# Second feed-forward block of a decoder layer: other chunk orders, six more mixed chunks, dense activations, another order of the last banks

## The chip, the cores and the metric

The kernel runs on one core of one Trainium2 chip. The metric is the device time of one execution in microseconds (us). It was run three times before the change: 2109.17, 2108.28 and 2108.98 us, a median of 2108.98 us.

## The reference

One layer of a decoder, for 256 tokens behind 16 learned meta tokens, in float32, with a width of 2048 and a hidden width of 5632:

```python
u = rms_norm(h, ffn1_norm_g[l])
h = h + 0.5 * swiglu(u, ffn1_w_gate[l], ffn1_w_up[l], ffn1_w_down[l])
u = rms_norm(h, mix_norm_g[l])
z = u @ w_in[l]
...                       # sparse attention, gated short convolution, merge
h = h + merged @ w_out[l]
u = rms_norm(h, ffn2_norm_g[l])
h = h + 0.5 * swiglu(u, ffn2_w_gate[l], ffn2_w_up[l], ffn2_w_down[l])
return h[:, N_META:]
```

with `swiglu(x, g, u, d) = (silu(x @ g) * (x @ u)) @ d`. The change lies almost wholly in the second `swiglu`, of which only the 256 tokens are computed.

## The kernel before, in words

Three stages follow each other: the first feed-forward block (`ffn_features`), the mixer (attention, convolution, merge, output projection), and the second feed-forward block (`ffn_tokens`). TensorE computes float32 products out of two rounded halves: each operand is split into a high part (`hi`, ScalarE, L175) and a rest (`lo`, VectorE, L176), and one product is three matmuls, hi by hi, hi by lo, lo by hi. In `ffn_tokens` this is `trio` (L408, L409, L410): the activations are the stationary operand of 128x128, the weights stream past in 512 columns. L409 is the matmul that reads the `lo` weights.

**Stream.** All weights pass through one `Stream`. It loads chunks of 128x2048 words from HBM on the SP queue into raw buffers (three, and a fourth, `raws`, in the second block), splits them piece by piece into `whi` and `wlo` (four buffers of 1024 columns each), and hands the pieces to TensorE in order. When TensorE's program comes to piece number `at`, `Stream.next` writes, in this order, the work put for the start of that piece (`first`), the split of the piece three further on, and the work put for its end (`waiting`):

```python
self.run(self.first, self.at)
if self.steps:
    self.steps.pop(0)()
self.split(self.at + 1 + self.ahead)
self.run(self.waiting, self.at)
```

So the order of each engine's list is fixed by piece numbers. `put(fns, slots)` counts in half pieces from now: slot 15 is the end of piece 7. A tuple of such slots for each kind of work stands in `LAG`. The split of a piece needs the buffer of the piece four before, which TensorE must have finished; this bounds how far VectorE and ScalarE can be ahead.

**The second block.** The 5632 hidden features are cut into eleven tiles of 512, in two groups of six and five. A tile multiplies the 256 tokens with 512 gate and 512 up columns, over 2048 rows: eight chunks of 256 rows (`quads`, with `gu` counting chunks). Behind the tiles of a group come two down passes (`d` = 0 and 2), each into 1024 output columns; their chunks are 256 hidden features each: twelve in the first group, ten in the second. I name the tiles of the first group tile 1 to 6, and the passes down 1 and down 2 (first group) and down 3 and down 4 (second group).

**Plain and mixed chunks.** A plain chunk is eight block products (two token halves, two row halves, two column halves), so 24 matmuls, in two pieces `0` and `1` of 12 matmuls each. A mixed chunk uses seven block products instead (Strassen's scheme in Winograd's form): 21 matmuls in four pieces, `A` (6), `B` (3, half a piece wide), `C` (6) and `D` (6). For it the stream loads 128x1536 words of the chunk and 128x2048 words of sums of its blocks. Those weight sums are made earlier, in `job`: load the chunk on the POOL queue, four VectorE additions (L568), store to a scratch tensor in HBM on the POOL queue. 57 such jobs run: 46 in the first block (`JOBS`), eleven in the merge part of the mixer. The sums of activations are made in `combos`: five additions (L702 to L706), then a split on ScalarE (L688) and VectorE (L689). Where these sums are kept, for the down passes, is in `homes`.

`MIXED` names the mixed chunks of a tile (1, 3, 5, 6; tile 1 has only 5, in `FIRST_MIXED`), `DOWN_MIXED` and `LAST_MORE` those of the down passes (6, 8, 9, 10 in both passes of the first group; 5, 6, 7 in down 3 and 3, 4, 5, 6, 7 in down 4). Within a tile or a pass the chunks run in rising order.

**Ends of tiles and passes.** Behind the last mixed chunk `spread` combines the banks of the extra products (L767 on ScalarE, L768 to L770 on VectorE). A down pass then adds into the residual: four operations of `halves_to` from the combined banks, and four of `gather_down` from the plain ones (all L840, one each of 128x512). In the second group `gather_down` also stores the output columns. `quads` with `tail` set runs the last chunk bank by bank, six matmuls each, in the order (first half of tokens, columns 0), (first, 1), (second, 0), (second, 1); the two banks of columns 0 lie in one tile, `three`.

The activations `act` of the second block lie in rows of 320 words (`PITCH`) of which 256 are used.

## Time and profile before

| | |
|---|---|
| runs, us | 2108.28, 2108.98, 2109.17 |
| span of the profiled execution | 2106.9 us, 2.1 us below the median of the runs |
| instructions | 31863, of which 12731 matmuls |
| DMA | 575.64 MB, mean 273 GB/s |
| first matmul of the second block | at 1418.94 us of the span |

The profile is one execution on the chip: a page with the busy time of each engine, forty equal slices, the DMA queues and the chain of work that ended last, and a trace that can be asked for single rows. PE is TensorE's matmuls, PEld its loads of the stationary operand, DVE is VectorE, ACT ScalarE, SP and POOL issue DMAs. A row of the timeline is: start, duration, engine, line, operation, out<-in with shapes, count, and in brackets the idle time before it with what ended it. Matmuls overlap: each is shown with 0.39 us though the next starts sooner, so PE is read by the starts of its rows and not by its busy time.

### The profile page before, as it was taken

The page shows a single profiled execution, that of the slowest core. Times are in us where ns is not written, and L with a number is a line of the kernel's source. Part 1 is how long each engine was busy: PE and PEld are TensorE (multiplying, and loading weights), DVE is VectorE, ACT ScalarE, POOL GpSimd, SP SyncE. Part 2 cuts the span into 40 slices and gives each one's busy share as a digit, 9 for nine tenths or more (in the row PEclk, how much of TensorE's full clock was granted, in tenths as well). Part 3 has the DMA queues.
Part 4 walks back from the last instruction along what each step waited for, and adds up shares of the span by engine and source line. Part 5 has one row for each costly group of instructions (what it writes and reads, how often), then busy time and mean ns, then how long its engine had stood idle before and what let it go on. Part 6 is the DMA issues. An engine that isn't in the chain of part 4 may idle for free.

```text
span 2106.9 us, 31863 instructions
## 1 busy us (share of the span) xinstructions
PE 2098.8 (100%) x12731; PEld 1889.9 (90%) x12731; DVE 1582.4 (75%) x2144; ACT 1058.9 (50%) x1342; POOL 106.0 (5%) x207
## 2 busy tenths in 40 slices
PE   9999999999999999999999999999999999999998
PEld 9999999999999999889988888888888888888887
DVE  7676766676776766578679678769788896878897
ACT  6444433344444445565444444456575565566654
POOL 0000000000000000000000000011000000000000
PEclk9999999999999999999999999999999999999999
DMA  7788888888888865445468886667988777799865
GB/s 265 260 320 327 324 315 322 311 337 310 322 313 325 328 224 177 164 159 181 152 216 329 323 301 223 219 233 255 314 314 300 281 268 247 282 306 319 306 250 207
DMA packets 85908, 575.64 MB, mean 273 GB/s; under 512 B 10112, under 2 KB 10880, under 8 KB 23808
## 3 DMA queue, kind: packets, MB, share of 16 engines
q1 hardware_dynamic: 64080, 438.34, 58.4%
q0 software_dynamic: 21104, 134.23, 17.1%
q8 instruction: 99, 1.62, 0.3%
q10 hardware_dynamic: 576, 1.05, 0.1%
q14 instruction: 49, 0.40, 0.1%
HBM read 504.90 MB, written 68.68 MB: 272 GB/s over the span
## 4 chain that ended last, share of the span: by engine, by line
PE 98%; DVE 1%; DMA 1%; issue 0%; ACT 0%; DVEq 0%; ACTq 0%
PE three L409 5%; PE three L408 5%; PE three L410 5%; PE pd L375 4%; PE pd L376 4%; PE pd L374 4%; PE pu L374 4%; PE pg L375 4%; PE pg L374 4%; PE pu L375 4%; PE pg L376 4%; PE pu L376 4%; PE pgt L402 3%; PE pgt L404 3%; PE pgt L403 3%; PE one L408 3%
## 5 line engine op out<-in xcount | busy, mean ns | idle before, releaser
L176 DVE TENSOR_TENSOR wlo<-raw,whi 128x1024 fp32r<-128x1024 f32 (+1 forms) x771 | 906.2, 1188 | 464.5 <-ACT whi L175 457.7
L175 ACT ACTIVATE whi<-raw 128x1024 fp32r<-128x1024 f32 (+1 forms) x771 | 786.4, 1030 | 883.4 <-PE pd L375 146.2
L375 PE MATMUL pd<-mid,whi 128*128 128x272 f32 x704 | 201.9, 287 | 0.0
L376 PE MATMUL pd<-mid,wlo 128*128 128x272 f32 x704 | 201.9, 287 | 0.0
L374 PE MATMUL pd<-mid,whi 128*128 128x272 f32 x704 | 201.9, 287 | 0.0
L374 PE MATMUL pu<-act,whi 128*128 128x272 f32 x672 | 192.8, 287 | 0.0
L376 PE MATMUL pu<-act,wlo 128*128 128x272 f32 x672 | 192.7, 287 | 0.0
L376 PE MATMUL pg<-act,wlo 128*128 128x272 f32 x672 | 192.7, 287 | 0.0
L375 PE MATMUL pg<-act,whi 128*128 128x272 f32 x672 | 192.7, 287 | 0.0
L375 PE MATMUL pu<-act,whi 128*128 128x272 f32 x672 | 192.7, 287 | 0.0
L374 PE MATMUL pg<-act,whi 128*128 128x272 f32 x672 | 192.7, 287 | 0.0
L568 DVE TENSOR_TENSOR made<-made 128x512 f32<-128x512 f32 x228 | 156.3, 685 | 0.0
L408 PE MATMUL three<-whi,act 128*128 128x512 f32 x352 | 137.2, 390 | 0.1
L409 PE MATMUL three<-wlo,act 128*128 128x512 f32 x352 | 137.0, 389 | 0.0
L410 PE MATMUL three<-whi,act 128*128 128x512 f32 x352 | 137.0, 389 | 0.0
L376 PEld LDWEIGHTS pd<-mid,wlo 128*128 128x128 f32 x704 | 132.7, 188 | 0.0
L374 PEld LDWEIGHTS pd<-mid,whi 128*128 128x128 f32 x704 | 132.7, 188 | 0.0
L375 PEld LDWEIGHTS pd<-mid,whi 128*128 128x128 f32 x704 | 132.7, 188 | 0.0
L176 DVE TENSOR_TENSOR wlo<-raws,whi 128x1024 fp32r<-128x1024 f32 x92 | 103.5, 1140 | 31.7 <-ACT whi L175 31.0
L374 PEld LDWEIGHTS pu<-act,whi 128*128 128x128 f32 x672 | 126.7, 188 | 0.0
L374 PEld LDWEIGHTS pg<-act,whi 128*128 128x128 f32 x672 | 126.7, 188 | 0.0
L376 PEld LDWEIGHTS pg<-act,wlo 128*128 128x128 f32 x672 | 126.6, 188 | 0.0
(381 smaller groups left out, 4482.7 us busy)
## 6 DMA issues: line engine op xcount, KB each, us to landing
raw<-in_wgu_dram SPq DMA_DIRECT2D x123, 1024.0 KB, 6.4
raw<-in_wd_dram SPq DMA_DIRECT2D x63, 1024.0 KB, 6.7
made<-in_wgu_dram POOLq DMA_DIRECT2D x41, 1024.0 KB, 10.6
made<-made POOLq DMA_DIRECT2D x41, 1024.0 KB, 6.5
raw<-made SPq DMA_DIRECT2D x31, 1024.0 KB, 6.1
raw<-in_wcv_dram SPq DMA_DIRECT2D x24, 1024.0 KB, 4.9
raw<-in_wgc_dram SPq DMA_DIRECT2D x24, 1024.0 KB, 5.1
raw<-in_wga_dram SPq DMA_DIRECT2D x24, 1024.0 KB, 5.4
```

What stands on the lines that cost most here:

```text
L175: nc.scalar.activation(hi[:, :n], raw, AF.Copy)
L176: nc.vector.tensor_sub(lo[:, :n], raw, hi[:, :n].bitcast(F32))
L374: nc.tensor.matmul(ps, whi, xhi, start=first, stop=False)
L375: nc.tensor.matmul(ps, whi, xlo, start=False, stop=False)
L376: nc.tensor.matmul(ps, wlo, xhi, start=False, stop=last)
L402: nc.tensor.matmul(ps, xhi, whi, start=k + i == 0, stop=False)
L403: nc.tensor.matmul(ps, xhi, wlo, start=False, stop=False)
L404: nc.tensor.matmul(ps, xlo, whi, start=False, stop=k + i == n - 1)
L408: nc.tensor.matmul(ps, x(0), w[0], start=first, stop=False)
L409: nc.tensor.matmul(ps, x(0), w[1], start=False, stop=False)
L410: nc.tensor.matmul(ps, x(1), w[0], start=False, stop=last)
L568: getattr(nc.vector, f"tensor_{op}")(to, a, b)
```

## The change

The chunks of tile 1 and of each down pass get an order of their own (`FIRST`, `DOWN`), and `order` takes that list. Two more chunks are mixed in tile 1 (1 and 3), one more in down 1 (4), two more in down 2 (4 and 2), one more in down 4 (2). Their activation sums are all put in the first pass of a group, by longer slot lists; `start` puts the additions and the splits when its time comes. To have room for them, `act` is packed densely (256 words a row) at the front of its tile, and the rest of the tile holds two more sets of sums (`beyond`). 63 weight sums are made in place of 57: 46 in the first block as before, six at the start of the mixer (`MID_JOBS`, in the places where `qT` and half of `cs` lie later, which are therefore allocated later), eleven in the merge part as before. The last chunk's banks run in the order (first, 0), (second, 0), (first, 1), (second, 1), and the output follows them.

```diff
-FIRST_MIXED = 5,
+FIRST_MIXED = 5, 1, 3
+FIRST = 0, 2, 4, 5, 1, 6, 3, 7
-LAST_MORE = 3, 4
-DOWN_MIXED = {6: (6, 8, 9, 10), 5: (5, 6, 7)}
+MID_JOBS = 6
+MID_FROM = 3
+MID_EVERY = 5
+DOWN = {
+    (0, 0): (0, 1, 2, 3, 5, 6, 8, 7, 9, 10, 4, 11),
+    (0, 2): (0, 6, 8, 1, 9, 10, 3, 4, 2, 5, 7, 11),
+    (1, 0): (0, 1, 2, 3, 4, 5, 6, 8, 7, 9),
+    (1, 2): (0, 5, 6, 1, 7, 4, 8, 3, 2, 9),
+}
+DOWN_MIXED = {(0, 0): (6, 8, 9, 10, 4), (0, 2): (6, 8, 9, 10, 4, 2), (1, 0): (5, 6, 7), (1, 2): (5, 6, 7, 4, 3, 2)}
...
-    below=(12, 17, 22, 30, 34), below_split=(15, 20, 30, 34, 35), fifth=(22, 25), late_below=(0, 5),
-    late_split=(0, 6),
+    below={0: (12, 17, 22, 30, 40, 48), 1: (12, 17, 22, 30, 38, 46)},
+    below_split={0: (15, 20, 30, 34, 45, 53), 1: (15, 20, 30, 35, 43, 49)},
...
+    flat = act.rearrange("p k i t -> p (k i t)")
+    dense = flat[:, : KD * 2 * SEQ].rearrange("p (k i t) -> p k i t", k=KD, i=2)
+    beyond = flat[:, KD * 2 * SEQ :][:, : 2 * 3 * 2 * P].rearrange("p (n q i t) -> p n q i t", n=2, q=3, i=2)
...
-                        (c[j, q], of(k + u, j), 2 * u + 1 - q) for j in (1, 2) for q in range(2) for u in range(2)
+                        (c[j, q], of(k + u, j), 2 * u + 1 - q) for q in range(2) for j in (1, 2) for u in range(2)
...
-            def homes(g, n):
-                if g or n < 3:
-                    return [halves[:, 3 * n : 3 * n + 3, :, 0] if g else below[:, n]]
+            def home(g, n):
+                if g:
+                    return halves[:, 3 * (n % 5) : 3 * (n % 5) + 3, :, n // 5]
+                if n < 3:
+                    return below[:, n]
+                if n > 3:
+                    return beyond[:, n - 4]
...
-                return [lambda j=j, q=q: one(j, q) for j in (1, 2) for q in (0, 1)]
+                return [lambda j=j, q=q: one(j, q) for q in (0, 1) for j in (1, 2)]
...
-                for q, (i, *slots) in enumerate(zip(DOWN_MIXED[n], LAG["below"], LAG["below_split"])):
-                    fns = down_combos(g, q, i)
-                    first = fns[0]
-                    fns[0] = lambda first=first, i=i, g=g: ([known(("mid", g, i // 2, j), 0) for j in range(2)], first())
-                    put(fns, 5 * (slots[0],) + (len(fns) - 5) * (slots[1],))
+                every = (*DOWN_MIXED[g, 0], *(i for i in DOWN_MIXED[g, 2] if i not in DOWN_MIXED[g, 0]))
+                for q, (i, *slots) in enumerate(zip(every, LAG["below"][g], LAG["below_split"][g])):
+                    def start(q=q, i=i, slots=slots, base=st.at, g=g):
+                        for j in range(2):
+                            known(("mid", g, i // 2, j), 0)
+                        fns = down_combos(g, q, i)
+                        for fn, at in zip(fns, 5 * (slots[0],) + (len(fns) - 5) * (slots[1],), strict=True):
+                            (st.waiting if at % 2 else st.first).append((base + at // 2, fn))
+                    st.put(start, slots[0] - 2)
...
+        for i, (src, to) in enumerate(made[JOBS : JOBS + MID_JOBS]):
+            job(
+                lambda i=i: mp.tile([P, RAW], F32, name="made", tag=("tB", "c1")[i % 2]), src, to,
+                st.at + MID_FROM + i * MID_EVERY, MID_EVERY, i < 2,
+            )
```

Three places of VectorE's list carry the prediction. The lines of the changed kernel are shifted: L171 is the split that was L176, L705 to L709 are the additions L702 to L706, L692 is L689, L1488 is L1469, L850 is L840.

**VectorE in tile 1, around pieces 10 to 15** (of 18 before, 22 now), before:

```order
L689 TENSOR_TENSOR act<-few,act 128x128
L689 TENSOR_TENSOR comb<-few,comb 128x3x128
L176 TENSOR_TENSOR wlo<-raws,whi 128x1024
L176 TENSOR_TENSOR wlo<-raws,whi 128x512
L1469 SCALAR_TENSOR_TENSOR act<-mt,small,act 128x128 x8
L176 TENSOR_TENSOR wlo<-raw,whi 128x1024
```

and now:

```order
L692 TENSOR_TENSOR act<-few,act 128x128
L692 TENSOR_TENSOR comb<-few,comb 128x3x128
L171 TENSOR_TENSOR wlo<-raws,whi 128x1024
L171 TENSOR_TENSOR wlo<-raws,whi 128x512
L1488 SCALAR_TENSOR_TENSOR act<-mt,small,act 128x128 x8
L171 TENSOR_TENSOR wlo<-raw,whi 128x1024
```

Nothing moved in this list, and the five additions stand behind the last row in both; but before, these pieces belonged to chunk 5 behind five plain chunks (120 matmuls), and now they belong to chunk 1 behind three plain chunks and the mixed chunk 5 (93 matmuls).

**VectorE in down 3, at the end of chunk 6** (`raws` are its pieces C and D), before:

```order
L176 TENSOR_TENSOR wlo<-raws,whi 128x1024 x2
L689 TENSOR_TENSOR mid<-few,mid 128x128
L689 TENSOR_TENSOR act<-few,act 128x3x128
L176 TENSOR_TENSOR wlo<-raw,whi 128x1024
L176 TENSOR_TENSOR wlo<-raw,whi 128x512
```

and now (`raw`, the two rows of 1024 ahead of the sums, are C and D):

```order
L171 TENSOR_TENSOR wlo<-raw,whi 128x1024 x2
L692 TENSOR_TENSOR mid<-few,mid 128x128
L692 TENSOR_TENSOR act<-few,act 128x3x128
L705 TENSOR_TENSOR few<-mid 128x512
L706 TENSOR_TENSOR few<-few 128x128
L707 TENSOR_TENSOR few<-few 128x128
L708 TENSOR_TENSOR few<-few 128x128
L709 TENSOR_TENSOR few<-few 128x128
L171 TENSOR_TENSOR wlo<-raw,whi 128x1024 x3
```

The five additions for chunk 4 now stand ahead of the split of the next piece. Down 1 has the same rows at the same piece (its chunks 8 and 7, with `below` for `act`).

**VectorE at the start of down 4**, before:

```order
L769 TENSOR_TENSOR u<-two,u 128x512
L770 TENSOR_TENSOR u<-three,u 128x2x512
L176 TENSOR_TENSOR wlo<-raw,whi 128x1024
L840 SCALAR_TENSOR_TENSOR first<-u,rcol,first 128x512 x4
L176 TENSOR_TENSOR wlo<-raw,whi 128x1024 x2
L840 SCALAR_TENSOR_TENSOR first<-three,rcol,first 128x512
```

and now:

```order
L692 TENSOR_TENSOR act<-few,act 128x3x128
L779 TENSOR_TENSOR u<-two,u 128x512
L780 TENSOR_TENSOR u<-three,u 128x2x512
L171 TENSOR_TENSOR wlo<-raw,whi 128x1024
L850 SCALAR_TENSOR_TENSOR first<-u,rcol,first 128x512 x4
L850 SCALAR_TENSOR_TENSOR first<-three,rcol,first 128x512 x2
L850 SCALAR_TENSOR_TENSOR first<-one,rcol,first 128x512
L850 SCALAR_TENSOR_TENSOR first<-two,rcol,first 128x512
L171 TENSOR_TENSOR wlo<-raw,whi 128x512
```

Before, the first split row shown is the first piece of chunk 0, and the eight additions into the residual stood in two lots of four with splits of plain pieces between them; now all eight stand between pieces A (the 1024 row) and B (the 512 row) of chunk 5, the second chunk of the pass.

More of the change, by code (lines that the diff above doesn't have):

```diff
@@ L291, in tile_decoder_layer @@
         for f in range(n):
-            now = sorted((*MIXED, *(FIFTH,) * ((g, f) in FIVE))) if gu else FIRST_MIXED
+            now, chunks = (MIXED, range(8)) if gu else (FIRST_MIXED, FIRST)
+            now = [i for i in chunks if i in now]
             sums = {i: scratch.tile([P, RAW], F32, name=f"made{gu + i}") for i in now}
             made += [(wgu2[gu + i], x) for i, x in sums.items()]
-            for i, name in order(8, now):
+            for i, name in order(chunks, now):
                 st.add_part(name, wgu2[gu + i], sums.get(i))
@@ L410, in trio, with quads @@
         nc.tensor.matmul(ps, x(1), w[0], start=False, stop=last)
-    def quads(c, m, x, mixed, n, after_mixed, tail=False):
+    def quads(c, m, x, mixed, chunks, after_mixed, tail=False):
         def of(k, j):
@@ L417, in quads @@
         plan, joined = [], []
-        for i, name in order(n, mixed):
+        last_mixed = [i for i in chunks if i in mixed][-1]
+        for i, name in order(chunks, mixed):
             k = 2 * i
@@ L552, in start_tiles, with job @@
         return four
-    def job(pool, bufs, src, to, at, every, touch):
+    def job(place, src, to, at, every, touch):
         box = {}
         def load():
-            box["x"] = pool[0].tile([P, RAW], F32, name="made", bufs=bufs)
+            box["x"] = place()
             if touch:
@@ L677, in ffn_tokens @@
             st.more_raw = [fp.tile([P, RAW], F32, name="raws") for _ in range(MORE_RAW)]
-            below = fp.tile([P, min(len(DOWN_MIXED[6]), 3), 3, 2, P], F32R, name="below")
-            halves = act[:, :, :, LATER + META :].rearrange("p k i (j t) -> p k i j t", j=2)
+            below = fp.tile([P, 3, 3, 2, P], F32R, name="below")
+            halves = dense.rearrange("p k i (j t) -> p k i j t", j=2)
             middle = mid.rearrange("p k i (j t) -> p k i j t", j=2)
@@ L876, in ffn_tokens @@
                     now = {i: mixed[i] for i in (MIXED if f or g else FIRST_MIXED)}
-                    if (g, f) in FIVE:
-                        now[FIFTH] = fifth
-                    if (g, f) == (g, 1 - g) and any(at[0] == g for at in FIVE):
-                        written.discard("fifth")
-                        fns = combos(halves, FIFTH, [below[:, 1, :1], below[:, 0]], "fifth")
-                        put(fns, 5 * (LAG["fifth"][0],) + 4 * (LAG["fifth"][1],))
-                    quads(c, m, lambda k, j, part: known(("act", k // 4), act_tokens(k, j, part)), now, 8, lambda m=m: put(spread(m), LAG["spread"]))
+                    chunks = tuple(range(8)) if f or g else FIRST
+                    quads(c, m, lambda k, j, part: known(("act", k // 4), dense[:, k, part, (j - 1) * P : j * P]), now, chunks, lambda m=m: put(spread(m), LAG["spread"]))
                     put(gather(x, c), LAG["gather"])
@@ L1375, in tile_decoder_layer @@
         st.later(jobs_pool, 3)
-        for i, (src, to) in enumerate(made[JOBS:]):
-            job(jobs, 2, src, to, st.at + LATE_FROM + i * LATE_EVERY, LATE_EVERY, i < 2)
+        for i, (src, to) in enumerate(made[JOBS + MID_JOBS :]):
+            job(
+                lambda: jobs[0].tile([P, RAW], F32, name="made", bufs=2), src, to,
+                st.at + LATE_FROM + i * LATE_EVERY, LATE_EVERY, i < 2,
+            )
         m = [mp.tile([P, 2, 2, 512], F32, name=f"m{i}", tag=t) for i, t in enumerate(("tA", "tB"))]
@@ L1463, in to_act @@
                 hi, lo = (
-                    act[:, d, i, LATER + META :][:, :SEQ].rearrange("p (j r b) -> p j r b", j=2, r=4) for i in range(2)
+                    dense[:, d, i].rearrange("p (j r b) -> p j r b", j=2, r=4) for i in range(2)
                 )
```

61 lines of the change are left out of this document (28 added, 33 removed).

## The prediction

> **What bounds the kernel now.** I read the page first, then the waits of TensorE, then its rows in the second block.
>
> ```profile
> PE 2098.8 (100%) x12731; PEld 1889.9 (90%) x12731; DVE 1582.4 (75%) x2144; ACT 1058.9 (50%) x1342; POOL 106.0 (5%) x207
> PEclk9999999999999999999999999999999999999999
> PE 98%; DVE 1%; DMA 1%; issue 0%; ACT 0%; DVEq 0%; ACTq 0%
> 1800.00:1900.00 100.00, 100.00 (x443) 82.78 (x442) 80.01 (x81) 61.07 (x68) 5.49 (x10) 1.00 0.87 302
> ```
>
> TensorE is the bound: busy throughout, at full granted clock, and 98% of the chain. The last row (a window: PE, PEld, DVE, ACT, POOL busy with counts, clock, DMA share, GB/s) gives the price of a matmul of 512 columns: 100 us / 443 = 0.226 us. So a matmul less is worth 0.226 us, and a wait of TensorE more costs its length. Where does it wait now?
>
> ```profile
> 2080.92 0.39 PE L409 MATMUL three<-wlo,mid 128*128 128x512 f32 x1
> 2083.43 0.39 PE L410 MATMUL three<-whi,mid 128*128 128x512 f32 x1
> 2027.66 0.39 PE L408 MATMUL three<-whi,mid 128*128 128x512 f32 x1
> 2028.41 0.50 PE L409 MATMUL three<-wlo,mid 128*128 128x512 f32 x1 [0.36 <-DVE wlo L176]
> 2028.74 0.40 PE L410 MATMUL three<-whi,mid 128*128 128x512 f32 x1
> 1796.10 0.39 PE L409 MATMUL three<-wlo,act 128*128 128x512 f32 x1
> 1797.38 0.39 PE L410 MATMUL three<-whi,act 128*128 128x512 f32 x1
> ```
>
> From start to start: 2.51 us for four steps, 1.08 for two and 1.28 for four, where steps of 0.226 would be 0.90, 0.45 and 0.90. So three waits, of 1.6 us (down 4), 0.6 us (down 3) and 0.4 us (first tile of the second group); at other places of the second block I found none. What ended the second is VectorE (its bracket). What ended the first is a load, which in the chain of waits took 8.25 us from its issue:
>
> ```profile
> DVE wlo L176 <- ACT whi L175: 488.7, 456, 3.6
> 2072.36 8.25 DMA raw<-sums
> 1418.90:1443.60 24.70, 24.70 (x110) 20.46 (x110) 21.15 (x49) 16.13 (x28) 2.73 (x5) 1.00 0.76 255
> 1443.60:1461.80 18.20, 18.20 (x82) 15.05 (x82) 17.91 (x33) 11.23 (x16) 0.00 (x0) 1.00 0.70 239
> 1666.00:1728.50 62.50, 62.50 (x277) 51.79 (x276) 58.22 (x87) 37.10 (x46) 0.00 (x0) 1.00 0.69 248
> 1728.50:1791.10 62.60, 62.60 (x277) 51.84 (x277) 43.73 (x44) 32.19 (x33) 0.00 (x0) 1.00 0.70 247
> 1995.70:2027.60 31.90, 31.90 (x142) 26.46 (x141) 31.13 (x53) 17.51 (x21) 0.00 (x0) 1.00 0.50 176
> ```
>
> Over the whole program VectorE has idle time to spare: the first row is the list of waits, 488.7 us of waiting for the high halves, which harm nobody. By stage it has not: 39.1 of 42.9 us in tile 1 (first two windows), 58.2 of 62.5 us in down 1, 43.7 of 62.6 us in down 2, 31.1 of 31.9 us in the first part of down 3. There it is the second bound, a few microseconds ahead of TensorE, and this change gives it more to do and TensorE less. The DMA engines stand at 50 to 76% there.
>
> **What the change removes.** Six mixed chunks of 21 matmuls in place of 24: 18 matmuls x 0.2267 = **-4.1 us** (0.2267 is the step from 1418.94 to 1443.42 us, 108 steps, rows below). The wait of 1.6 us in down 4 came at the fourth of five mixed chunks in a row, each with two loads; now there are never more than two in a row there. I take it as gone, **-1.6**; it could stay (0). The 0.4 us at 1796 came from the residual additions of down 2, of which half now fall inside down 2, behind three plain chunks: **-0.4**.
>
> **What it adds, place by place.** The durations are VectorE's, as starts of consecutive rows in down 3:
>
> ```profile
> 2025.47 0.69 DVE L702 TENSOR_TENSOR few<-mid 128x512 f32<-128x512 f32 x1
> 2027.13 1.82 DVE L176 TENSOR_TENSOR wlo<-raw,whi 128x1024 fp32r<-128x1024 f32 x2
> 2028.87 2.36 DVE L176 TENSOR_TENSOR wlo<-raws,whi 128x1024 fp32r<-128x1024 f32 x2
> 2031.14 0.29 DVE L689 TENSOR_TENSOR mid<-few,mid 128x128 fp32r<-128x128 f32 x1
> 2031.81 6.36 DVE L176 TENSOR_TENSOR wlo<-raw,whi 128x1024 fp32r<-128x1024 f32 x6
> 2033.32 0.39 PE L409 MATMUL three<-wlo,mid 128*128 128x512 f32 x1
> 2044.20 2.73 DVE L840 SCALAR_TENSOR_TENSOR first<-u,rcol,first 128x512 f32<-128x512 f32 x4
> ```
>
> Five additions take 1.66 us (2025.47 to 2027.13), a pair of splits of sums 0.67 (2031.14 to 2031.81), a split of 1024 columns 1.13 ((2031.14 - 2028.87) / 2), of 512 columns 0.6 (the rest of 1.74), a residual addition 0.67.
>
> *Tile 1.* VectorE's list is the same as before up to piece 13 but for one split that is half as wide, so its clock is that of the trace, 0.5 us earlier. Piece 13 is D, once of chunk 5, now of chunk 1:
>
> ```profile
> 1442.47 2.19 DVE L1469 SCALAR_TENSOR_TENSOR act<-mt,small,act 128x128 fp32r<-128x128 f32 x8
> 1447.56 3.60 DVE L176 TENSOR_TENSOR wlo<-raw,whi 128x1024 fp32r<-128x1024 f32 x3
> 1418.94 0.39 PE L408 MATMUL one<-whi,act 128*128 128x512 f32 x1
> 1443.42 0.39 PE L408 MATMUL one<-whi,act 128*128 128x512 f32 x1
> ```
>
> The split of piece 13 starts at 1447.56 and ends 1.13 later, at 1448.7; now at about 1448.2. Ahead of D stand 93 + 15 = 108 matmuls now, 135 before: without waits D begins at 1443.42 and its first L409 at 1443.65. So TensorE must have lost 4.6 us by then, in pieces (5D 0.9, 1A 0.3, 1C 2.0, 1D 1.4, by adding VectorE's rows from 1427.8 on), 4.7 with restarts. The cover of before, six microseconds of plain chunks, is what the earlier mixed chunks take away. From both sides: 0 if the rows ahead of 1442.47 could start that much earlier, 6.1 (27 matmuls) if VectorE were no earlier at all. I take **+4.7**.
>
> *Down 3.* Before, the split behind the pair starts at 2031.81 and ends at 2032.94, and TensorE reads it at 2033.32 without a wait. Now the five additions stand between: 2031.81 + 1.66 + 1.13 = 2034.6, a wait of 1.3, with the restart 1.4: **+1.4**. The 0.6 us at 2027.66 stays, its rows are the same.
>
> *Down 1.* Its pieces 9 to 18 now have the rows that down 3 has; before, it had a plain chunk there, and no wait. So it gets the 0.6 us and the 1.4 us of down 3. Then the sums for chunks 4 and 2 fall into 9, 10 and 4, three mixed chunks in a row. From the end of the second wait to the split of 10D VectorE has seven splits of 1024 (7.9), two of 512 (1.2), four short splits of sums for chunk 10 (0.9), a pair (0.7) and two lots of additions (3.3): 14.0 us. TensorE is there after 60 matmuls, 13.6 us. With what follows in 4C, 0.6. Together **+2.6**, between 0 and 4.
>
> *Down 2.* Its second chunk is mixed now, with the residual additions of down 1 before A to D. That is the pattern that the first tile of the second group had, with its 0.4: **+0.4**.
>
> *Down 4.* From the wait in down 3 on, VectorE has, to the split of 5B: nine splits of 1024 (10.2), two of 512 (1.2), three pairs (2.0), two lots of additions (3.3), the combination of the banks (2.3: rows of 512, 512 and 1024) and eight residual additions (5.3), 24.3 us. TensorE has chunks 8, 7, 9, 0 and piece 5A ahead of it, 99 matmuls or 22.4 us. A wait of 1.9, 0.1 for the restart, and 0.4 in 5C behind it: **+2.4**, between 0 and the eight additions' 5.3. Before, the plain chunks 0, 1 and 2 stood there. In each of these places the instruction that waits is an L409, and TensorE's whole list is behind it; nothing fills such a wait.
>
> *Weight sums in the mixer.* Six jobs of four additions:
>
> ```profile
> L568 DVE TENSOR_TENSOR made<-made 128x512 f32<-128x512 f32 x228 | 156.3, 685 | 0.0
> 797.00:897.00 100.00, 100.00 (x562) 85.60 (x561) 63.48 (x137) 51.28 (x75) 0.53 (x2) 1.00 0.51 174
> 830.00:850.00 20.00, 20.00 (x93) 16.59 (x92) 16.94 (x60) 11.37 (x19) 0.00 (x0) 1.00 0.55 197
> ```
>
> 24 x 0.685 = 16.4 us on VectorE beside 63.5 of 100 us, and 12.6 MB of DMA at half load. The tightest 20 us hold some four additions, 16.9 + 2.7 = 19.7 of 20. The lead of the splits hides it: 0, at most 2 if a transfer comes late (a job's load waits on POOL for the store two jobs before it, and its additions hold VectorE's list till the load has landed). Dense activations: rows with `mid` (dense) and `act` (spaced) both step by 0.23 us above: 0.
>
> *The end.*
>
> ```profile
> 2096.95 2.73 DVE L840 SCALAR_TENSOR_TENSOR first<-u,rcol,first 128x512 f32<-128x512 f32 x4
> 2100.20 0.75 DVE L840 SCALAR_TENSOR_TENSOR first<-three,rcol,first 128x512 f32<-128x512 f32 x1 [0.53 <-PE three L410]
> 2102.19 0.74 DVE L840 SCALAR_TENSOR_TENSOR first<-two,rcol,first 128x512 f32<-128x512 f32 x1
> ```
>
> The 0.53 us goes, since both halves of `three` end earlier. But only one chunk now follows the last mixed one, where two did, so the combination and the first row's four additions begin 5.4 us later against TensorE's end, with less to split beside them: +0.1, between -0.5 and +1.
>
> **The sum.** -4.1 - 1.6 - 0.4 + 4.7 + 2.6 + 0.4 + 1.4 + 2.4 + 0.1 = **+5.5 us**: 2106.9 becomes 2112.4 in the profiled execution. The median of the runs lies 2.1 us above the span; 2109.0 + 5.5 = **2114.5 us**. 0.2% (4.2 us) is about what a measurement here can tell from no change.
>
> **Rivals.** *Faster.* VectorE's idle time in the second block (20 of 100 us in the window from 1800) covers the bunches after all, because it gets further ahead than I added up; then only the savings count, 2109.0 - 6.1 = 2102.9. For it: VectorE is never full over a whole pass but in down 3. Against: the three rows of down 3 that already wait. Chance 0.16. *About the same.* One large term fails, tile 1 or the pair down 3 and 4, which leaves 2109.8 to 2110.7. The change would then buy matmuls with waits one for one. Chance 0.22. *Slower by loads.* A mixed chunk loads 1.84 MB in 4.76 us, 386 GB/s.
>
> ```profile
> 2081.50:2083.50 2.00, 0.94 (x4) 0.55 (x4) 1.69 (x2) 2.00 (x3) 0.00 (x0) 1.00 1.01 424
> ```
>
> The DMA engines reach 424 GB/s when they are behind, and three mixed chunks in a row ran before in down 1 without a wait. But if each of the three passes with more mixed chunks waits once as at 2081, with 1.6 us, it is 2114.5 + 4.8 = 2119.3. It decides as soon as a load takes over 8 us instead of 6. Chance 0.07. (The Trainium skill, "DMA: Bandwidth & Descriptors", section Specifications, gives about 358 GB/s as the limit from HBM for a core; by it three mixed chunks in a row, 5.5 MB, take 15.4 us as an estimate against 14.3 us of TensorE, and this rival would be the likeliest. The 424 GB/s of the row speak against that.)
>
> **Chances.** The forecast (2111 to 2118) 0.55. Slower by over 0.2% (above 2113.2): most of the forecast and the loads, 0.56. Within 0.2%: the rest of the forecast and the second rival, 0.28. Faster: 0.16. The range leaves out the faster rival and the worst of the loads: 2105 to 2119.
>
> **What would show it.** Right: waits of TensorE for `wlo` in tile 1 at about 25 us from its start (near 4.7 us together), in down 1 and 3 behind the first two mixed chunks, in down 4 at the second chunk; 18 matmuls fewer. Wrong: steps of 0.227 us through tile 1, or waits that a load ends.

## The result, and the profile after

The changed kernel takes **2119.93 us** (median of four runs, 2119.04 to 2120.54) against 2108.63 us (2107.85 to 2109.17) for the kernel before on the same chip: 11.3 us more, a ratio of 1.0055 with a 95% interval of 1.0041 to 1.0069. The direction was forecast, the size was twice the forecast of 5.5 us, and the time lies 0.9 us above the upper end of the range. The profiled execution spans 2118.8 us, 11.9 more than before.

The page of the changed kernel, its lines on busy engines, on the granted clock and on the chain that ended last:

```profile
PE 2100.1 (99%) x12713; PEld 1886.0 (89%) x12713; DVE 1613.6 (76%) x2203; ACT 1070.1 (51%) x1360; POOL 112.3 (5%) x219
PEclk9999999999999999999999999999999999999999
PE 91%; DVE 6%; issue 1%; DMA 1%; ACT 1%; DVEq 0%; SPq 0%; ACTq 0%
```

The 18 matmuls are gone (12731 to 12713) and TensorE still fills the span, but its share of the chain fell from 98% to 91%, and VectorE's rose from 1% to 6%. The list of waits of TensorE names the places where that happened (us in total, times, longest):

```profile
PE one L408 <- DVE wlo L171: 2.5, 2, 1.3
PE two L408 <- DVE wlo L171: 2.3, 3, 1.1
PE three L408 <- DVE wlo L171: 2.2, 3, 1.5
PE three L407 <- DVE u L780: 2.0, 1, 2.0
PE three L407 <- DVE first L850: 0.3, 1, 0.3
```

Eight waits for `wlo`, where the same list of before has two, of 1.1 us together; and two of another kind: a first matmul (L407) that waits for `u`, in down 4, and one that waits for an addition into the residual (L850), in down 2. The stages that got longer, as windows (PE, PEld, DVE, ACT, POOL, clock, DMA share, GB/s), tile 1, down 1 and down 3; first before, then after:

```profile
1418.94:1461.78 42.84, 42.84 (x191) 35.49 (x189) 39.04 (x80) 27.37 (x44) 2.73 (x5) 1.00 0.73 248
1665.98:1728.54 62.56, 62.56 (x277) 51.81 (x276) 58.28 (x87) 37.10 (x46) 0.00 (x0) 1.00 0.69 248
1995.70:2048.74 53.04, 52.68 (x233) 43.30 (x231) 52.07 (x76) 30.58 (x36) 0.00 (x0) 1.00 0.65 237
```

```profile
1421.84:1467.93 46.09, 42.71 (x184) 34.04 (x183) 41.74 (x83) 30.06 (x48) 2.74 (x5) 1.00 0.76 265
1672.45:1737.60 65.15, 62.96 (x275) 50.93 (x273) 63.59 (x103) 39.84 (x52) 0.00 (x0) 1.00 0.68 244
2003.53:2058.16 54.63, 53.01 (x232) 43.20 (x231) 52.87 (x88) 32.42 (x42) 0.00 (x0) 1.00 0.63 225
```

In down 1 VectorE is busy for 63.6 of 65.2 us: it is the bound there, as the prediction said. In tile 1 it is busy for 41.7 of 46.1 us and TensorE waits all the same, since the extra work comes in bunches: from 1436.00 to 1451.10 us it is busy for 13.6 of 15.1 us. The waits stand at the L408 rows (the bracket is the idle time ahead of the row and what ended it), three in tile 1 and three in down 1. A fourth step of tile 1, at 1444.38, is 0.3 us too long and has no bracket:

```profile
1442.58 0.50 PE L408 MATMUL two<-wlo,comb 128*128 128x512 f32 x1 [0.62 <-DVE wlo L171]
1448.22 0.50 PE L408 MATMUL three<-wlo,act 128*128 128x512 f32 x1 [1.50 <-DVE wlo L171]
1451.02 0.50 PE L408 MATMUL two<-wlo,comb 128*128 128x512 f32 x1 [1.12 <-DVE wlo L171]
1705.16 0.50 PE L408 MATMUL three<-wlo,mid 128*128 128x512 f32 x1 [0.36 <-DVE wlo L171]
1711.49 0.50 PE L408 MATMUL one<-wlo,mid 128*128 128x512 f32 x1 [1.24 <-DVE wlo L171]
1725.98 0.50 PE L408 MATMUL two<-wlo,sum 128*128 128x512 f32 x1 [0.59 <-DVE wlo L171]
```

Start to start each of these waits costs some 0.27 us more than its bracket says, because a shown matmul lasts 0.39 us where a step is 0.227, and because the next step takes 0.34 us. So I measure each stage by the start of its first matmul, the same matmul in both traces:

| stage, us | before | after | difference | forecast |
|---|---|---|---|---|
| first 600 matmuls | 79.67 | 81.14 | +1.47 | 0 |
| from there to the second block | 1339.27 | 1340.70 | +1.43 | 0 |
| tile 1 | 42.84 | 46.09 | +3.25 | +3.34 |
| tiles 2 to 6 | 204.20 | 204.52 | +0.32 | 0 |
| down 1 | 62.56 | 65.15 | +2.59 | +1.92 |
| down 2 | 62.57 | 61.73 | -0.84 | -0.96 |
| tiles of the second group | 204.59 | 204.20 | -0.39 | -0.40 |
| down 3 | 53.04 | 54.63 | +1.59 | +1.40 |
| down 4, to its last matmul | 52.40 | 54.36 | +1.96 | +0.12 |
| from there to the end | 5.76 | 6.28 | +0.52 | +0.10 |

The column of forecasts is the prediction's sum, with the saved matmuls (six in tile 1, three in down 1, six in down 2, three in down 4) put where they are saved. It adds up to +5.5, the measured one to +11.9. Of the 6.4 us between them 1.8 lie in down 4, 1.5 in the first 600 matmuls, 1.4 between these and the second block, 0.7 in down 1, 0.4 at the end, 0.3 in tile 2 and 0.2 elsewhere.

At the start of down 4 VectorE's rows and TensorE's two around the wait:

```profile
2055.37 1.23 DVE L171 TENSOR_TENSOR wlo<-raw,whi 128x1024 fp32r<-128x1024 f32 x1
2056.51 0.68 DVE L778 TENSOR_TENSOR u<-one,u 128x512 f32<-128x512 f32 x1
2057.11 1.22 DVE L171 TENSOR_TENSOR wlo<-raw,whi 128x1024 fp32r<-128x1024 f32 x1
2058.62 0.39 PE L409 MATMUL one<-whi,mid 128*128 128x512 f32 x1
2058.92 0.69 DVE L779 TENSOR_TENSOR u<-two,u 128x512 f32<-128x512 f32 x1
2059.64 1.22 DVE L780 TENSOR_TENSOR u<-three,u 128x1024 f32<-128x1024 f32 x1
2061.01 0.47 PE L407 MATMUL three<-whi,mid 128*128 128x512 f32 x1 [2.00 <-DVE u L780]
```

The matmul at 2061.01 writes the bank tile `three` which L780, the last step of the combination of down 3's banks, has to read first. VectorE came to it at 2059.64. The step is 2.39 us long, 2.16 more than without a wait, and it is not the wait that I forecast for chunk 5. Behind it, from 2062.36 to 2065.77, the windows in the last section show TensorE at half its clock.

At the end (`after`, last matmul and VectorE's last additions):

```profile
2112.52 0.39 PE L409 MATMUL two<-whi,mid 128*128 128x512 f32 x1
2110.13 2.73 DVE L850 SCALAR_TENSOR_TENSOR first<-u,rcol,first 128x512 f32<-128x512 f32 x4
2112.78 1.40 DVE L850 SCALAR_TENSOR_TENSOR first<-three,rcol,first 128x512 f32<-128x512 f32 x2
2114.76 0.74 DVE L850 SCALAR_TENSOR_TENSOR first<-two,rcol,first 128x512 f32<-128x512 f32 x1
```

Nothing waits for TensorE here: VectorE runs without a gap and begins its last addition 2.24 us after the last matmul has begun.

### The profile page after: what moved, and what is told of

Its sections match the earlier page's. It is cut to its first block, busy times and chain, and to the rows that moved or that the text cites. A ratio compares the mean times of both kernels' runs of the same rounds, so it can differ in the third digit from the quotient of the medians.

```text
span 2118.8 us, 31963 instructions
## 1 busy us (share of the span) xinstructions
PE 2100.1 (99%) x12713; PEld 1886.0 (89%) x12713; DVE 1613.6 (76%) x2203; ACT 1070.1 (51%) x1360; POOL 112.3 (5%) x219
## 4 chain that ended last, share of the span: by engine, by line
PE 91%; DVE 6%; issue 1%; DMA 1%; ACT 1%; DVEq 0%; SPq 0%; ACTq 0%
PE three L407 4%; PE three L408 4%; PE three L409 4%; PE pd L375 4%; PE pd L374 4%; PE pd L373 4%; PE pu L374 4%; PE pg L374 4%; PE pg L373 4%; PE pu L373 4%; PE pu L375 4%; PE pg L375 4%; PE pgt L401 3%; PE pgt L402 3%; PE pgt L403 3%; DVE wlo L171 3%
## 5 line engine op out<-in xcount | busy, mean ns | idle before, releaser
L171 DVE TENSOR_TENSOR wlo<-raw,whi 128x1024 fp32r<-128x1024 f32 (+1 forms) x779 | 912.8, 1184 | 469.7 <-ACT whi L170 464.2
L568 DVE TENSOR_TENSOR made<-made 128x512 f32<-128x512 f32 x252 | 172.7, 685 | 2.8 <-DMA made<-in_wgu_dram 2.8
L408 PE MATMUL three<-wlo,act 128*128 128x512 f32 x352 | 137.3, 390 | 1.7 <-DVE wlo L171 1.5
L407 PE MATMUL three<-whi,act 128*128 128x512 f32 x352 | 137.0, 389 | 0.0
L409 PE MATMUL three<-whi,act 128*128 128x512 f32 x352 | 136.9, 389 | 0.0
L373 PEld LDWEIGHTS pg<-act,whi 128*128 128x128 f32 x672 | 126.6, 188 | 0.0
L373 PEld LDWEIGHTS pu<-act,whi 128*128 128x128 f32 x672 | 126.6, 188 | 0.0
L374 PEld LDWEIGHTS pu<-act,whi 128*128 128x128 f32 x672 | 126.6, 188 | 0.0
L374 PEld LDWEIGHTS pg<-act,whi 128*128 128x128 f32 x672 | 126.6, 188 | 0.0
```

Of the source, the lines that this page charges most:

```text
L171: nc.vector.tensor_sub(lo[:, :n], raw, hi[:, :n].bitcast(F32))
L373: nc.tensor.matmul(ps, whi, xhi, start=first, stop=False)
L374: nc.tensor.matmul(ps, whi, xlo, start=False, stop=False)
L407: nc.tensor.matmul(ps, x(0), w[0], start=first, stop=False)
L408: nc.tensor.matmul(ps, x(0), w[1], start=False, stop=False)
L409: nc.tensor.matmul(ps, x(1), w[0], start=False, stop=last)
```

## The experiments

Theory: what was lost is VectorE's work in places where its lead over TensorE is short, and each place can be mended by itself. Rivals: the lag is only handed on from place to place; the loss lies in the loads, or in the mixer. Times are medians, each beside the kernel before on the same chip (2108.9 to 2109.2 us); stages come from the traces.

**Tile 1 as before** (`tile1_old`, against the changed kernel):

```diff
-FIRST_MIXED = 5, 1, 3
-FIRST = 0, 2, 4, 5, 1, 6, 3, 7
+FIRST_MIXED = 5,
+FIRST = 0, 1, 2, 3, 4, 5, 6, 7
```

> The changed kernel with tile 1 as before: rising order, only chunk 5 mixed (61 weight sums in place of 63). Theory A, VectorE is the bound in tile 1 and the three mixed chunks there cost more than they save: the waits of about 4.9 us at 1441 to 1450 us go, six matmuls (1.36 us) come back, so 2119.9 - 4.9 + 1.4 = 2116.4 us. Rival B, VectorE's lag is only handed on, and the same waits come up in the next tile or in down 1: 2119.9 + 1.4 = 2121 us, or little below 2119.9.

2116.05 us (2115.43 to 2116.94), 3.9 us less than the changed kernel. No wait is left in tile 1, tiles 2 to 6 take 204.20 us as before the change, and down 1 to down 4 each take what they took in the changed kernel, within 0.2 us. So of the lag only the 0.3 us in tile 2 were handed on; theory A holds. Two more mixed chunks, in the order they need, cost tile 1 3.3 us net.

**Late sums in down 4** (`late_sums`, against the changed kernel):

```diff
-    below={..., 1: (12, 17, 22, 30, 38, 46)},
-    below_split={..., 1: (15, 20, 30, 35, 43, 49)},
+    below={..., 1: (12, 17, 22, 30, 72, 80)},
+    below_split={..., 1: (15, 20, 30, 35, 77, 85)},
```

> The changed kernel, with the activation sums of chunks 3 and 2 made in down 4 itself (slots 72 and 80) in place of the end of down 3. The two lots of additions and splits, 2 x (1.66 + 0.67) = 4.7 us of VectorE, no longer stand ahead of the combination of down 3's banks. Theory A, TensorE's wait of 2.2 us at the first matmul of down 4 is that lag of VectorE, and the eight or so matmuls at half speed behind it (1.5 us) come from the wait: both go, 2119.9 - 3.7 = 2116.2 us, and no step above 0.3 us at the start of down 4. Rival B, the wait is in the order itself, since the combination now comes one plain chunk before the pass ends and cannot be earlier: most of it stays, 2118 us or more. Rival C, the half speed is no consequence of the wait: the wait goes, the slow steps stay, 2117.7 us.

2117.20 us (2116.81 to 2117.70), 2.7 us less. The wait at the first matmuls of down 4 is gone and so are the slow steps behind it, so B and C fall. The gain is 1 us short of A, since other waits came up behind: 0.8 us at chunk 1, and 0.8 us at chunk 4, where the additions for chunk 2 now stand ahead of a split. The first of these is a load. ScalarE's row at chunk 1, and TensorE's:

```profile
2071.13 2.01 ACT L170 ACTIVATE whi<-raw 128x1024 fp32r<-128x1024 f32 x2 [2.03 <-DMA raw<-in_wd_dram]
2073.50 0.50 PE L408 MATMUL one<-wlo,mid 128*128 128x512 f32 x1 [0.51 <-DVE wlo L171]
```

ScalarE had nothing to split for 2.03 us until a transfer landed, and TensorE then waits for VectorE, which waits for ScalarE. So two mixed chunks in a row (5 and 6) are enough here to make the load of the plain chunk behind them late.

**Bank order alone** (`tail_only`, the kernel before with the two lines of the diff on the last banks):

```diff
-                        (c[j, q], of(k + u, j), 2 * u + 1 - q) for j in (1, 2) for q in range(2) for u in range(2)
+                        (c[j, q], of(k + u, j), 2 * u + 1 - q) for q in range(2) for j in (1, 2) for u in range(2)
...
-                return [lambda j=j, q=q: one(j, q) for j in (1, 2) for q in (0, 1)]
+                return [lambda j=j, q=q: one(j, q) for q in (0, 1) for j in (1, 2)]
```

> The kernel before with nothing but the new order of the last chunk's banks and of the stores behind them. By the prediction the wait of 0.53 us at the end goes: 2108.1 us, between 2108.0 and 2108.7. Rival: the stores of the last columns now come closer together, and the end is 0.5 us longer, as the changed kernel's end is (6.3 us from the last matmul's start to the end of the span, 5.8 before): 2109.1 us.

2108.19 us against 2109.17, ratio 0.9997 (0.9989 to 1.0006): the time can't tell it from no change. In the trace the end takes 5.0 us (span 2105.0, last matmul at 2100.02) where it took 5.8, so the bank order gains about 0.8 us in this trace, and the longer end of the changed kernel has another cause. Only 0.6 us of the gain is VectorE's: in the three traces with this bank order and the chunks of before (this one, `mixer_new` and `shim`) its last addition ends 1.2 us after the last matmul has begun, in the three with the old order 1.8 us. What follows the last addition, the last store among it, takes 3.8 us here, and in `shim` 4.8, so that there the end takes 6.0 us in spite of the new order.

**The mixer alone** (`mixer_new`, the changed kernel with the second block as before):

```diff
+FIRST_MIXED = 5,
+FIRST = 0, 1, 2, 3, 4, 5, 6, 7
+DOWN = {(0, 0): range(12), (0, 2): range(12), (1, 0): range(10), (1, 2): range(10)}
+DOWN_MIXED = {(0, 0): (6, 8, 9, 10), (0, 2): (6, 8, 9, 10), (1, 0): (5, 6, 7), (1, 2): (5, 6, 7, 3, 4)}
...
+    below={..., 1: (12, 17, 22, 52, 57)},
+    below_split={..., 1: (15, 20, 30, 52, 58)},
```

> The changed kernel with the second block's chunk orders, mixed chunks and slots as before (57 weight sums, six of them still made at the start of the mixer, five in the merge part; dense activations and the new bank order stay). By the prediction all that is left costs nothing: 2108.6 us, as the kernel before or as the one with the bank order alone. Rival: what the changed kernel lost ahead of the second block (1.5 us in its first 30 us, 1.4 us between 1135 and 1420 us) belongs to these parts, and it is 2110 to 2111.5 us; if the first 1.5 us are chance, 2110.

2108.98 us against 2109.17, no difference that the time can tell. The trace says more: from matmul 600 to the second block it takes 1340.70 us, as in the changed kernel, and 1339.3 with the bank order alone. This is no chance of one trace: the six traces with the new mixer and no further edit to it have 1340.6 to 1340.8 us, the three with the mixer of before 1339.3. So 1.4 us are lost in the mixer, by a part that I had put at nothing, and the bank order hides most of it in the total. The 1.5 us of the first 600 matmuls are chance: over the fourteen traces, which all begin with the same 600 matmuls, they take 79.6 to 81.1 us, and 80.2 here.

**The kernel before, once more** (`before_again`, no edit):

> The kernel before, unchanged, for a second profile. The prediction counted two waits of its first profile as savings: 1.6 us at the fourth mixed chunk of down 4 (a load) and 0.4 us in the first tile of the second group. If they belong to the kernel, both stand in this profile too, within 0.1 us. If they were chance of one execution, they are shorter here, as in the kernel with the bank order alone, where the first was about 0.3 us and the second 0.06.

2107.88 us. The waits that the prediction had booked as savings are smaller in this execution. Down 4's fourth mixed chunk:

```profile
2081.39 0.39 PE L408 MATMUL three<-whi,mid 128*128 128x512 f32 x1
2082.26 0.50 PE L409 MATMUL three<-wlo,mid 128*128 128x512 f32 x1 [0.48 <-DVE wlo L176]
```

0.87 us from start to start and 0.34 for the next step, so about 0.75 us of waiting where the first profile had 1.6; with the bank order alone it was 0.3. In the first tile of the second group less than 0.1 us is left of 0.4, while `shim`, with the same second block but for the order of the last banks, waits there for 0.8 us. The wait of 0.6 us in down 3 is the same in all of them. So of the 2.0 us that I counted as saved, 1.2 to 1.6 were chance of one execution.

**Addresses** (`shim`, against `mixer_new`; `before_off`, against the kernel before):

```diff
+        mp.tile([P, 32], F32, name="shim")
         for i, (src, to) in enumerate(made[JOBS : JOBS + MID_JOBS]):
...
+            if c == 0:
+                mp.tile([P, 32], F32, name="shim2")
             if c % 4 == 0:
                 cs.append(mp.tile([P, KC // 2, 2, SEQ], F32R, name=f"cs{c // 4}", tag=f"c{c // 4}"))
```

```diff
+        mp.tile([P, 32], F32, name="shim")
         zz = [mp.tile([P, 1024], F32, name=f"zz{j}", tag=f"zz{j}") for j in range(2)]
```

> The changed kernel with the second block's orders and slots as before (as in mixer_new), and two unused tiles of 128 bytes a partition, put so that qT and the two halves of cs (and the merged activations that follow them in the same places) start at multiples of 256 bytes again, as they do in the kernel before; in the changed kernel qT and one half of cs start 128 bytes off. Theory A, matmuls whose stationary operand lies 128 bytes off take 0.233 us in place of 0.227 us, and that is what the mixer lost: from matmul 600 of the trace to the first matmul of the second block it takes 1339.4 us as before, not 1340.7. Rival B, it is the six sums at the start of the mixer or the DMA beside the merge part: 1340.7 us remain.

> The kernel before with one unused tile of 128 bytes a partition at the front of the mixer's pool, and nothing else: every tile of that pool moves by 128 bytes, so all stationary operands of the merge and the output projection out of cs, ys and ms (768 matmuls by the loops) start 128 bytes off a multiple of 256, where in mixer_new one half of cs and of ms did (192 matmuls, 1.1 us). Theory A, it is the address of the stationary operand: 768 x 0.006 us = 4.5 us more between matmul 600 and the first matmul of the second block (1343.9 us in place of 1339.4), 2113.4 us in all. Rival B, what the two unused tiles of the run named shim changed was something else (the distance between tiles, or which transfer lies beside which): no change, 2108.9 us.

With the two unused tiles the stretch from matmul 600 to the second block takes 1339.57 us, and in the three `best` runs below, which have these tiles too, 1339.6: 1.1 of the 1.4 us are back. Matmul 600 and the first of the second block, `mixer_new` and then `shim`:

```profile
80.17 0.29 PE L370 MATMUL pg<-act,wlo 128*128 128x272 f32 x1
1420.87 0.39 PE L402 MATMUL one<-whi,act 128*128 128x512 f32 x1
79.91 0.29 PE L370 MATMUL pg<-act,wlo 128*128 128x272 f32 x1
1419.48 0.39 PE L402 MATMUL one<-whi,act 128*128 128x512 f32 x1
```

The time does not show it: the one execution of `shim` took 2109.15 us, since it had 1.2 us of waits at the starts of down 2 and of the second group, and the long end told above. And one unused tile in the kernel before takes 3.75 us: 2112.74 us (2111.82 to 2113.85) against 2108.99, ratio 1.0018 (1.0009 to 1.0027); the stretch is 1343.42 us where it was 1339.31. Theory A holds in both directions. The first matmul of the output projection and the first behind it, `before_again` and then `before_off`:

```profile
1331.90 0.39 PE L402 MATMUL po<-whi,ms 128*128 128x512 f32 x1
1419.27 0.39 PE L408 MATMUL one<-whi,act 128*128 128x512 f32 x1
1334.24 0.40 PE L402 MATMUL po<-whi,ms 128*128 128x512 f32 x1
1423.49 0.40 PE L408 MATMUL one<-whi,act 128*128 128x512 f32 x1
```

The same 384 matmuls take 87.37 and 89.25 us, 0.2275 and 0.2324 each (the former with 0.3 us of waits in it). The places are those that the program's allocation gives to the tiles; a profile does not print them. The last 0.3 us of the 1.4 appear in one step at 822 us, where the mixer starts; what does that was not tried.

**Down 1 as before** (`down1_free`, against the changed kernel):

```diff
-    (0, 0): (0, 1, 2, 3, 5, 6, 8, 7, 9, 10, 4, 11),
+    (0, 0): range(12),
-DOWN_MIXED = {(0, 0): (6, 8, 9, 10, 4), ...
-    below={0: (12, 17, 22, 30, 40, 48), ...
-    below_split={0: (15, 20, 30, 34, 45, 53), ...
+DOWN_MIXED = {(0, 0): (6, 8, 9, 10), ...
+    below={0: (12, 17, 22, 30, 88, 96), ...
+    below_split={0: (15, 20, 30, 34, 93, 101), ...
```

> The changed kernel with down 1 as before (rising order, chunks 6, 8, 9, 10 mixed, no further sums); chunks 4 and 2 are mixed in down 2 as in the changed kernel, their sums made in down 2 (slots 88 and 96). Theory A, VectorE is full in down 1 and has room in down 2: the waits of down 1 (3.3 us in the trace) go, three matmuls (0.7 us) come back, 2119.9 - 2.6 = 2117.3 us. Rival B, the two lots of sums cost in down 2 what they cost in down 1: a new wait of 1 us or more there, 2118.5 us or more.

2117.51 us (2117.09 to 2118.20), 2.4 us less. Down 1 has no wait, and down 2 gets one of 0.86 us at chunk 10, where a lot of five additions stands ahead of the split of piece D. So A, with a remainder.

**Two plain chunks at the end** (`two_plain`, against the changed kernel):

```diff
-    (1, 2): (0, 5, 6, 1, 7, 4, 8, 3, 2, 9),
+    (1, 2): (0, 5, 6, 1, 7, 4, 3, 2, 8, 9),
```

> The changed kernel with chunk 8 of down 4 moved back by two places (order 0, 5, 6, 1, 7, 4, 3, 2, 8, 9), so that two plain chunks follow the last mixed one. Theory A: the end, 6.3 us from the start of the last matmul, was long because VectorE still had the combination and eight additions to do; it becomes about 5 us, 2119.9 - 1.3 = 2118.6 us. Rival B: four mixed chunks in a row wait for a load as the five of before did in some executions, 0.3 to 1.4 us, and most of the gain goes: 2119 to 2120 us.

2118.27 us (2117.78 to 2119.34), 1.7 us less, and the end takes 4.3 us (span 2116.0, last matmul at 2111.72). The fourth mixed chunk in a row waits for 0.3 us only. VectorE's last addition ends 1.2 us after the last matmul has begun, in the changed kernel 3.0. So the end was VectorE's, as A says.

**Putting it together** (`best1`, `best2`, `best3`, each against the changed kernel; tile 1 and down 1 as before, the two unused tiles, and for `best3`):

```diff
...
+    (0, 2): (0, 1, 6, 8, 3, 9, 10, 5, 4, 2, 7, 11),
+    (1, 0): range(10),
+    (1, 2): (0, 5, 1, 6, 7, 2, 4, 3, 8, 9),
+DOWN_MIXED = {(0, 0): (6, 8, 9, 10), (0, 2): (6, 8, 9, 10, 4, 2), (1, 0): (5, 6, 7), (1, 2): (5, 6, 7, 4, 3)}
+    below={0: (12, 17, 22, 30, 84, 104), 1: (12, 17, 22, 60, 80)},
+    below_split={0: (15, 20, 30, 34, 87, 109), 1: (15, 20, 30, 63, 83)},
...
```

`best1` differs by down 4 (0, 5, 1, 6, 2, 7, 4, 8, 3, 9) and by the slots of the late sums (92 and 100, 64 and 76); `best2` by slots 82 and 78 for 84 and 80, and by a late second mixed chunk in tile 1 (order 0, 1, 2, 4, 5, 6, 3, 7), with the split of its sums two half pieces earlier.

> What the runs so far allow, together: tile 1, down 1 and down 3 as before; chunks 4 and 2 mixed in down 2 with their sums made in down 2; down 4 with the mixed chunks of before (3 to 7) but a plain chunk between most of them, its late sums made in down 4; the new bank order, and the two unused tiles that put cs and qT back on 256 bytes. Theory A: against the 2109.0 us of mixer_new, six matmuls less (1.4 us), 1.3 us of the mixer back, no wait for a load in down 4 (0.3 us or more): 2106 us. Rival B: the sums in down 2 and down 4 bring waits of 1 to 2 us, or the addresses are not what cost the mixer 1.3 us: 2107.5 to 2109 us.

2108.01 us against 2108.91 (ratio 0.9995, 0.9986 to 1.0004), not told from no change; rival B. Down 4 has no wait at all, but chunk 10 of down 2 waits for 0.86 us, the end takes 6.5 us with one plain chunk behind the last mixed one, and tile 3 shows a wait of 0.8 us that no other trace has there.

> best1 with four edits: two plain chunks behind the last mixed one of down 4 (order 0, 5, 1, 6, 7, 2, 4, 3, 8, 9) in place of one; the sums made in down 2 and down 4 put ahead of splits of plain pieces, not ahead of those of mixed ones; one chunk more mixed in tile 1 (3, late, order 0, 1, 2, 4, 5, 6, 3, 7, where its sums are made in any case). Theory A: the end of best1 took 6.45 us from the last matmul's start, since VectorE came out of the combination and its eight additions late; with two plain chunks behind it takes about 5 us, as in the kernel with the bank order alone; the wait of 0.86 us at chunk 10 of down 2 goes; three matmuls less (0.7 us): 2108.0 - 1.4 - 0.9 - 0.7 = 2105.0 us. Rival B: VectorE is as full in tile 1 with one late mixed chunk as with three, and a wait of 0.7 us or more comes there, and three mixed chunks within four wait for a load in down 4 as before: 2106.5 us or more.

2108.15 us against 2108.99 (ratio 0.9996, 0.9987 to 1.0005), rival B again: the end is 4.5 us as expected and chunk 10 of down 2 waits no more, but tile 1 and the start of tile 2 wait for 3.3 us in place of the 0.7 saved, and down 2 and down 4 for 0.5 us each at the first piece of a plain chunk. The wait at the start of tile 2 is again one for L780, as at the start of down 4:

```profile
1446.81 0.50 PE L408 MATMUL one<-wlo,act 128*128 128x512 f32 x1 [0.72 <-DVE wlo L171]
1464.59 0.47 PE L407 MATMUL three<-whi,act 128*128 128x512 f32 x1 [1.31 <-DVE u L780]
```

So one late mixed chunk more brings 3.3 us of waits, where the two more of the changed kernel brought 4.8 (tile 1 and the start of tile 2).

> best2 with tile 1 as before (only chunk 5 mixed) and the additions of the late sums one half piece later in down 2 (84 for 82) and down 4 (80 for 78), so that they stand ahead of the second split of a plain chunk and not of the first. Theory A: the second mixed chunk of tile 1 cost 3.2 us of waits there and at the start of tile 2 for 0.7 us saved, and the two waits of 0.5 us in down 2 and down 4 are those additions: 2108.15 - 2.5 - 0.9 = 2104.7 us. Rival B: the waits only move on by a piece: 2105.6 us.

**2105.04 us** (2104.44 to 2106.04) against 2108.86, ratio 0.9976 (0.9958 to 0.9994): 0.2% less than the kernel before, and each of its eleven runs is below the fastest of that kernel beside them (2107.61). It lies between A and B, and the trace decides for A. All waits of TensorE in it:

```profile
PE warm L366 <- POOL ones L325: 1.0, 1, 1.0
PE start L375 <- DVE wlo L171: 0.5, 1, 0.5
PE three L408 <- DVE wlo L171: 0.3, 1, 0.3
PE start L373 <- ACT whi L170: 0.2, 1, 0.2
```

Only the third lies in the second block; it is the 0.6 us of down 3 that the kernel before has too. Stage by stage against `before_again`, down 2 with six matmuls less takes 1.3 us less, down 4 without a wait 0.8 and the end 1.2, while the mixer still takes 0.3 more and the first 600 matmuls 0.2. That makes the 3.0 us between the two traces (2106.1 and 2103.1 us); the medians are 3.8 us apart.

## Why the prediction was right and wrong

**Right: VectorE is the second bound, and the mixed chunks buy matmuls with waits.** The 18 matmuls went. Tile 1 (+3.25 against a forecast of +3.34) and down 3 (+1.59 against +1.40) came out within 0.2 us, each at the place that was named and with VectorE's split ending the wait. Here the working held: take the trace's times, move VectorE's list as the order shows it, and compare with TensorE's matmuls. `tile1_old` and `down1_free` show that the costs of tile 1 and down 1 belong to their places.

**Right in its size, not in its reason: down 2**, -0.84 against -0.96. The wait came at the start of its second chunk, as forecast, but at its first matmul into `three` and not at an L409 of the old numbering, the matmul that reads the `lo` weights. The addition L850 still had to read that bank. The wait of before that the forecast was copied from was of the same kind: the additions that read `three` end at 1796.70, and the first matmul into it begins at 1796.84. Changed kernel, then two rows of before:

```profile
1743.46 0.47 PE L407 MATMUL three<-whi,mid 128*128 128x512 f32 x1 [0.26 <-DVE first L850]
1795.29 1.41 DVE L840 SCALAR_TENSOR_TENSOR first<-three,rcol,first 128x512 f32<-128x512 f32 x2
1796.84 0.47 PE L408 MATMUL three<-whi,act 128*128 128x512 f32 x1
```

**Too small: down 1**, +2.59 against +1.92. The two waits copied from down 3 came as said (0.63 and 1.5 us); the wait at chunk 10 was 0.86 us where I had added up 0.4 for it. Each stop also costs some 0.11 us at the step behind it, of which my sums held only part.

**Wrong in its place, and too small: down 4.** The prediction summed VectorE's work up to the split of 5B and found it 1.9 us late there, +2.4 in all. But TensorE stands still before that: its first matmul into `three` needs L780 to be done, and of the rows shown above the prediction for this place L780 is the third, ahead of the eight additions. I had asked only when the weights would be ready, not when the bank would be free. Measured were some 4.2 us: 2.2 at the bank, 1.6 in the steps at half clock behind it and 0.4 at a load. `late_sums` shows the cause, the two lots of sums ahead of the combination: without them the wait is gone.

**Wrong: two savings that were chance of one execution.** The -1.6 for the load in down 4 and the -0.4 in the second group stood in the profile, but `before_again` has 0.75 and 0.1 us there. The table above is laid against that same first profile, so it still books them. And the wait for a load did not go for good: "never more than two in a row" was not enough, as `late_sums` (0.8 us at chunk 1) shows, and the changed kernel has 0.36 us of it.

**Wrong: the mixer at nothing.** It lost 1.4 us. The prediction priced the six jobs and the density of `act`, and passed over the sentence of the change that moves `qT` and half of `cs` to other places. It is the place that costs: 1.1 us, shown by `shim` and `before_off`. The six jobs themselves cost 0.3 us at most, and whether that is theirs stays open.

**Wrong in its mechanism: the end.** It is +0.5 us, inside the bounds given, but as a sum of -0.8 for the bank order (`tail_only`) and about +1.3 to +2.0 for the missing plain chunk behind the last mixed one (`two_plain`: 6.3 to 4.3 us). I had seen that one chunk follows where two did, and priced it at +0.6.

**The rivals.** The faster one is out: every place with a mixed chunk more and no more cover waits. So is the one with a large term missing: tile 1, down 3 and down 4 all cost about what was forecast or more. The loads were not the large term: TensorE's waits in the second block of the changed kernel end with VectorE, and only down 4's 0.36 us goes back to a transfer. The figure of the Trainium skill weighed there (the limit from HBM in "DMA: Bandwidth & Descriptors", section Specifications) would have made three mixed chunks in a row a bound; four in a row cost 0.3 us in `two_plain`.

Of the 11.3 us, the single repairs give back 3.9 (tile 1), 2.4 (down 1), 2.7 (late sums), 1.7 (the end) and 1.1 (addresses, by the trace), 11.8 together; each counts the matmuls that come back with it. The five were not run together on the changed kernel, and part of the 11.3 us is the first 600 matmuls and other chance; but no large part is left without a name.

## What to carry to other kernels

A cheaper operation that shifts work to the second engine pays only where that engine has lead in that very stretch: here the same kind of chunk was worth its 0.7 us in down 2 of `best3` and cost 1.6 us net in tile 1, and its sums were free ahead of the second split of a plain chunk and cost 0.5 to 0.9 us elsewhere. When an engine's list is moved, ask of the waited-for engine not only when its operands are ready but also when its output bank is free, and leave enough plain work behind the last special unit of a pass. Before a wait is booked as a saving, look at a second profile of the same kernel, and print where tiles lie when an edit moves an allocation.

## What the runs showed of the hardware that I had not expected

**The address of the stationary operand.** Matmuls of 128x128 by 128x512 whose stationary operand starts 128 bytes off a multiple of 256 take 0.2324 us from start to start, on the average of the 768 steps of `cs`, `ys` and `ms` in `before_off`, and 0.2267 us when it does not, in `before_again` (without two steps that hold waits). Within one execution it shows too: in the changed kernel the steps of `cs`, one half of which lies off, take 0.2299 us, those of `ys`, all of which lies on such multiples, 0.2267. Other offsets were not tried.

**Half clock after a wait of 2 us.** Windows of the changed kernel, of `tile1_old` and of `down1_free`, each with the stretch of 3.41 us that holds most of the wait at the start of down 4, and the next one (the second number, with its count, is PE's busy time; the granted clock is the 1.00 or 0.50):

```profile
2058.95:2062.36 3.41, 1.41 (x7) 1.17 (x7) 3.38 (x5) 0.10 (x1) 0.00 (x0) 1.00 0.81 303
2062.36:2065.77 3.41, 3.41 (x10) 2.62 (x9) 3.41 (x6) 1.06 (x1) 0.17 (x1) 0.50 0.03 10
```

```profile
2054.71:2058.12 3.41, 1.64 (x7) 1.41 (x8) 3.38 (x5) 0.00 (x0) 0.00 (x0) 1.00 0.85 308
2058.12:2061.53 3.41, 3.40 (x15) 2.45 (x14) 3.41 (x7) 1.06 (x1) 0.46 (x1) 1.00 0.01 2
```

```profile
2055.21:2058.62 3.41, 1.56 (x7) 1.00 (x6) 3.38 (x5) 0.47 (x1) 0.00 (x0) 1.00 0.77 286
2058.62:2062.03 3.41, 3.41 (x10) 2.63 (x9) 3.41 (x6) 1.06 (x1) 0.00 (x0) 0.50 0.05 22
```

The stretches are laid on the changes of the clock in each trace (in `tile1_old` on the one behind its last matmul) and counted on in steps of 3.41 us. The first stretch of each holds 1.4 to 1.7 us of work and the wait. With PE busy for 1.41 and 1.56 us of such a stretch the next one ran at half clock, for just 3.41 us; with 1.64 us it did not. Laid so over all fourteen traces, every stretch with PE busy for 1.56 us or less is followed by half clock (the others of these lie at the ends of the programs), and none with 1.64 us or more. The Trainium skill ("TensorE: Matmul & The Clock Gate", Part 1, What's actually happening) has a free-running window of 3413 ns and the half clock after at least one idle window; the length agrees, but here a window a little more than half idle was enough. It cost nothing that shows: to its last matmul down 4 takes 54.36 and 54.31 us in the changed kernel and in `down1_free`, and 54.36 and 54.25 us in `two_plain` and in `tile1_old`, where the clock stayed at 1.00. There TensorE waited for VectorE a little further on instead.
